# Modulation vectors by row sums on VectorE, state space weights on VectorE alone, and table loads counted as waits, in a two-layer diffusion backbone

## The chip, the cores and the metric

The kernel runs on one core of one Trainium2 chip. The metric is the device time of one execution in microseconds; the kernel before is shown with the median of three runs. A core has TensorE (matmuls, into PSUM), VectorE, ScalarE, GpSimd, and SyncE, which here issues every DMA. In the profile they are called PE (PEld is its loading of weights), DVE, ACT, POOL and SP.

## The reference

Two layers work on 384 tokens of 1024 features: 128 context tokens and 256 latent tokens. Each token set has a conditioning vector of its own, and each layer computes nine modulation vectors of 1024 from it, a shift, a scale and a gate for each of three sublayers:

```python
sc = jax.nn.silu(cond)
mod = sc @ w_ada[l] + b_ada[l]                    # 1024 -> 9 x 1024
sh1, sc1, g1, sh2, sc2, g2, sh3, sc3, g3 = split(mod, 9)
h = rmsnorm(x, norm_w[l, 0]) * (1 + sc1) + sh1
x = x + 0.5 * g1 * swiglu_a(h)                    # 1024 -> 2816 -> 1024
h = rmsnorm(x, norm_w[l, 1]) * (1 + sc2) + sh2
x = x + g2 * (concat(gla(h), delta_rule(h), s5(h)) @ w_out[l])
h = rmsnorm(x, norm_w[l, 2]) * (1 + sc3) + sh3
x = x + 0.5 * g3 * swiglu_b(h)
```

The third mixer (S5) is a diagonal state space in complex numbers. Its discretized weights (powers of the decay times b and c) depend on parameters alone, so they can be made before the mixer runs. All is in float32.

## The kernel before

**Tiling.** Activations lie transposed: a tile is 128 features by 384 tokens. Each 128x128 piece of a weight is multiplied in three passes: activations and weights are each split into a high and a low half that together have the accuracy of float32 (`mm3`: high x high, high x low, low x high). Each weight tile of 128x1024 thus needs ScalarE, which casts `raw` to its high half `wh`, and VectorE, which subtracts to get the low half `wl`. There are three `raw`, two `wh` and two `wl` tiles. TensorE needs about four microseconds for one tile.

**Stages.** The program runs FFN (0,0), mixer 0, FFN (0,2), FFN (1,0), mixer 1, FFN (1,2); the first number is the layer, the second the sublayer. An FFN has 22 products of gate and up (16 matmul triples each), each followed by SiLU, a product, and a split into `ph` and `pl`, and then 8 down projections of 22 triples. A norm stands between stages.

**Modulation.** The vectors are numbered by block (0 to 8 in each layer). The first two are made at the start on TensorE. The table `ADA` says for every stage which vectors it makes on the side (`now`) and which late (`late`). A side vector goes through `ada_side`: 8 loads of 128x1024 of `w_ada` (rows are inputs), and for each of the two conditionings an accumulation on VectorE, `asum <- araw * sT + asum`; the first of the eight is a scaled copy on ScalarE. What is left is a sum over partitions, which `ada_sum` does on TensorE with 8 matmuls against a one-hot constant; `ada_end` then copies on ScalarE, transposes twice on TensorE and adds the bias on VectorE. A late vector is multiplied whole on TensorE with 32 small matmuls, held back until the stage's last product, so that they fill TensorE while the norm runs. Eleven vectors are made on the side and five late; two of the late ones, (0,8) and (1,8), belong to the mixers.

**State space weights.** In the FFN ahead of each mixer, `s5_prep` makes powers and `s5_weights` makes, in four quarters, products of 128x512 and writes them to DRAM. `s5_weights` uses `self.vp`, an engine handle for which the planner may choose VectorE or GpSimd at each instruction.

**Order.** Every operation is recorded with the engines that it may run on, a planned cost and what it depends on; the planner `Plan` sets the order of each engine's queue with clocks of its own. It takes the operation that can start first (`when`), and among those that can start within 100 ns of it on the same engine the one of highest priority. Modulation's side work has the lowest priority (`side=-1`), the weight stream a high one (20). A function of another table set on ScalarE adds 1300 to the planned cost `c`, not to the planned start. `pace` and `calm` hold back the loads of side vectors by the FFN's progress and by the planned load of the DMA queue. Engines carry out their queues in order, so an instruction that waits holds back all behind it.

**Tiles.** `place` gives out the tiles of side work: six `araw` and three `asum` of 128x1024. The two running sums of a side vector are held `asum` tiles; the state space weights take theirs from `asum` as well.

## Time and profile before

| | |
|---|---|
| median of 3 runs | 1878.63 us (1873.07 to 1885.66) |
| profiled execution | 1874.38 us, its span from first to last instruction 1872.6 us |
| TensorE | busy 1794.6 us, granted clock 0.988 on average |
| VectorE, ScalarE, GpSimd | busy 1257.7, 791.4 and 294.3 us |
| chain that ended last | TensorE 72%, VectorE 16%, ScalarE 4%, DMA 4%, issue 3%, GpSimd 1% |

The chain that ended last is followed back from the end: at each step to what released the instruction, or to the one before it on its engine. 72% of it is TensorE, so TensorE sets the pace; where VectorE stands in it, TensorE waited for VectorE. A matmul's length is modelled, so that a busy TensorE can still have small gaps; the distance of equal instructions in the timeline tells more. All recorded operations have line 552, that of the planner's call, so groups are told apart by tile names: `wl<-raw,wh` is the low half of a weight, `s<-s,ps` and `pl<-s,ph` belong to a product of gate and up, `asum<-araw,sT,asum` is modulation's accumulation, `s5T` belongs to the state space weights.

### The profile page before, as it was taken

The page shows a single profiled execution, that of the slowest core. Times are in us where ns is not written, and L with a number is a line of the kernel's source. Part 1 is how long each engine was busy: PE and PEld are TensorE (multiplying, and loading weights), DVE is VectorE, ACT ScalarE, POOL GpSimd, SP SyncE. Part 2 cuts the span into 40 slices and gives each one's busy share as a digit, 9 for nine tenths or more (in the row PEclk, how much of TensorE's full clock was granted, in tenths as well). Part 3 has the DMA queues.
Part 4 walks back from the last instruction along what each step waited for, and adds up shares of the span by engine and source line. Part 5 has one row for each costly group of instructions (what it writes and reads, how often), then busy time and mean ns, then how long its engine had stood idle before and what let it go on. Part 6 is the DMA issues. An engine that isn't in the chain of part 4 may idle for free.

```text
span 1872.6 us, 33567 instructions
## 1 busy us (share of the span) xinstructions
PE 1794.6 (96%) x13626; PEld 1639.7 (88%) x13626; DVE 1257.7 (67%) x2061; ACT 791.4 (42%) x1357; POOL 294.3 (16%) x350
## 2 busy tenths in 40 slices
PE   8999999998999999999999999999999999999998
PEld 6988899887786779999988999997877768999997
DVE  4898885577895767666559777645989667444333
ACT  4533332465434553333254433335564355333332
POOL 1133240125110010000013125102342001000000
PEclk9999999999999999999999999999999999999999
DMA  9766677343110435556635565663421104333443
GB/s 285 264 211 205 221 237 240 116 146 110 49 35 24 158 113 181 194 167 192 226 124 175 188 207 190 199 218 131 134 87 49 35 23 170 124 124 125 129 124 96
DMA packets 111835, 282.05 MB, mean 151 GB/s; under 512 B 22656, under 2 KB 41408, under 8 KB 111680
## 3 DMA queue, kind: packets, MB, share of 16 engines
q1 hardware_dynamic: 111680, 279.90, 46.1%
q8 instruction: 107, 1.75, 0.4%
q14 instruction: 48, 0.39, 0.1%
HBM read 266.37 MB, written 13.48 MB: 149 GB/s over the span
## 4 chain that ended last, share of the span: by engine, by line
PE 72%; DVE 16%; ACT 4%; DMA 4%; issue 3%; POOL 1%; SPq 0%; DVEq 0%; POOLq 0%; ACTq 0%
PE ps L552 72%; DVE wl L552 4%; DVE asum L552 3%; DVE mM L552 2%; DVE s L552 2%; DMA araw<-in_wada 2%; DVE mZ L552 1%; ACT s L552 1%; DVE Ga L552 1%; ACT wh L552 1%; ACT h L552 1%; DMA wd<-asum 1%; DVE Gb L552 1%; DMA kd<-sC 0%; ACT mZ L552 0%
## 5 line engine op out<-in xcount | busy, mean ns | idle before, releaser
L552 ACT CAST wh<-raw 128x1024 fp32r<-128x1024 f32 (+1 forms) x332 | 341.7, 1030 | 701.6 <-PE ps L552 546.6
L552 PE MATMUL ps<-h,wl 128*128 128x384 f32 x1792 | 611.4, 341 | 15.0 <-DVE wl L552 14.5
L552 PE MATMUL ps<-h,wh 128*128 128x384 f32 x1792 | 612.8, 342 | 11.4 <-ACT h L552 9.9
L552 PE MATMUL ps<-l,wh 128*128 128x384 f32 x1792 | 610.9, 341 | 4.9 <-DVE l L552 3.9
L552 DVE TENSOR_TENSOR wl<-raw,wh 128x1024 fp32r<-128x1024 f32 (+1 forms) x332 | 414.0, 1247 | 264.2 <-ACT wh L552 263.8
L552 PEld LDWEIGHTS ps<-h,wl 128*128 128x128 f32 x1792 | 340.5, 190 | 25.3 <-DVE wl L552 21.7
L552 PEld LDWEIGHTS ps<-h,wh 128*128 128x128 f32 x1792 | 340.6, 190 | 23.2 <-ACT h L552 14.2
L552 PEld LDWEIGHTS ps<-l,wh 128*128 128x128 f32 x1792 | 340.4, 190 | 13.1 <-DVE l L552 9.3
L552 DVE SCALAR_TENSOR_TENSOR asum<-araw,sT,asum 128x1024 f32<-128x1024 f32 x154 | 204.8, 1344 | 57.4 <-DMA araw<-in_wada 56.7
L552 PE MATMUL ps<-ph,wl 128*128 128x384 f32 x704 | 237.6, 337 | 1.9 <-DVE wl L552 1.8
L552 PE MATMUL ps<-ph,wh 128*128 128x384 f32 x704 | 237.8, 338 | 0.0
L552 PE MATMUL ps<-pl,wh 128*128 128x384 f32 x704 | 237.4, 337 | 0.0
L552 PEld LDWEIGHTS ps<-ph,wl 128*128 128x128 f32 x704 | 132.2, 188 | 3.7 <-DVE wl L552 2.8
L552 PEld LDWEIGHTS ps<-ph,wh 128*128 128x128 f32 x704 | 132.2, 188 | 0.9 <-issue 0.6
L552 PEld LDWEIGHTS ps<-pl,wh 128*128 128x128 f32 x704 | 132.2, 188 | 0.4 <-issue 0.4
L552 POOL TENSOR_TENSOR s<-x,s 128x384 f32<-128x384 f32 x24 | 25.1, 1054 | 566.1 <-ACT s L552 520.2
L552 DVE TENSOR_TENSOR s<-s,ps 128x384 f32<-128x384 f32 x88 | 48.4, 551 | 79.4 <-PE ps L552 76.4
L552 PE MATMUL ps<-mZ,mM 64*64 64x128 f32 (+1 forms) x960 | 67.5, 267 | 6.9 <-DVE mM L552 4.0
L552 PEld LDWEIGHTS ps<-mZ,mM 64*64 64x64 f32 x960 | 53.2, 134 | 21.8 <-DVE mM L552 9.6
L552 ACT CAST ph<-s 128x384 fp32r<-128x384 f32 x88 | 44.6, 509 | 49.8 <-DVE s L552 49.6
L552 DVE SCALAR_TENSOR_TENSOR s<-s,p_small,s 128x392 f32<-128x392 f32 x96 | 61.9, 661 | 2.7 <-ACT s L552 1.8
L552 POOL TENSOR_TENSOR asum<-s5T,s5T 128x512 f32<-128x512 f32 x20 | 39.0, 1948 | 157.6 <-PE ps L552 99.0
(303 smaller groups left out, 2081.9 us busy)
## 6 DMA issues: line engine op xcount, KB each, us to landing
raw<-in_wgu SPq DMA_DIRECT2D x170, 512.0 KB, 3.9
araw<-in_wada SPq DMA_DIRECT2D x106, 512.0 KB, 4.9
raw<-in_wdn SPq DMA_DIRECT2D x64, 512.0 KB, 3.6
raw<-in_win SPq DMA_DIRECT2D x44, 512.0 KB, 3.5
raw<-in_wdn SPq DMA_DIRECT2D x32, 384.0 KB, 3.2
raw<-in_wout SPq DMA_DIRECT2D x16, 512.0 KB, 3.5
araw<-in_wada SPq DMA_DIRECT2D x22, 256.0 KB, 5.8
bd<-s SPq DMA_DIRECT2D x16, 256.0 KB, 4.1
```

Source lines behind the costliest of these rows:

```text
L552: getattr(self.eng[e], fn)(*a, **kw)
```

## The change

It has four parts.

1. A side vector is computed the other way round. The input holds `w_ada` once more, transposed (`wadaT`: 128 outputs by 1024 inputs in each block), and both conditioning vectors repeated over all partitions (`cR`). At the start of each stage two tiles take SiLU of `cR`. For each of 8 blocks and each conditioning, one VectorE instruction multiplies the block by that tile and writes the row's sum into a column of `adav` (`accum_out`). One addition of the bias ends the vector. The sum over partitions, the copy on ScalarE, the two transposes and the two additions are gone. The product itself isn't used; it goes to a tile `trash` or over the block.
2. The table `ADA` changes: (0,8) and (1,3) become side vectors of FFN (0,2), and (1,8) one of FFN (1,2). The mixers make none. Late are (0,5) and (1,5) alone. Fourteen vectors are made on the side.
3. `s5_weights` runs on VectorE alone, and its tiles come from the six `araw`, since the three `asum` are now held by `trash` and the two SiLU tiles.
4. In `when`, a change of table set adds its 1300 to the planned start, not to the cost.

```diff
@@ _pack
     o["wada"] = f(g["w_ada"])
+    o["wadaT"] = f(g["w_ada"].reshape(L, D, 9, KD, 128).transpose(0, 2, 3, 4, 1))
+    o["cR"] = f(np.broadcast_to(cc.T[None], (128, 2, D)))
@@ Plan.when
             if w[3] is not None and w[3] != self.table:
-                c += 1300.0
+                s += 1300.0
@@
 ADA = {(0, 0): ([(0, 2), (0, 3), (0, 4), (0, 6), (0, 7)], [(0, 5)]),
-       (0, 1): ([], [(0, 8)]),
-       (0, 2): ([(1, 0), (1, 1), (1, 2)], [(1, 3)]),
+       (0, 2): ([(0, 8), (1, 0), (1, 1), (1, 2), (1, 3)], []),
        (1, 0): ([(1, 4), (1, 6), (1, 7)], [(1, 5)]),
-       (1, 1): ([], [(1, 8)]),
-       (1, 2): ([], [])}
+       (1, 2): ([(1, 8)], [])}
@@ Kern.ada_side
-        acc = [raw(KD + s, True) for s in range(2)]
-        for k in range(KD):
+        v = self.t(pool, [128, KD, 2], "adav")
+        for d in range(KD):
             yield pace
             yield self.plan.calm()
             self.adan += 1
-            t = raw(k)
-            self.dma(out=t, in_=self.A["wada"][l, k * 128:(k + 1) * 128, b * 1024:b * 1024 + 1024])
+            t = self.place(pool, 0, False)
+            self.dma(out=t, in_=self.A["wadaT"][l, b, d])
             for s in range(2):
-                if k == 0:
-                    self.act(acc[s], t, AF.Copy, scale=self.sT[:, k, s:s + 1])
-                else:
-                    self.ve.scalar_tensor_tensor(acc[s], t, self.sT[:, k, s:s + 1], acc[s], ALU.mult, ALU.add)
-        self.plan.spawn(self.ada_sum(l, b, acc), 5)
+                self.ve.scalar_tensor_tensor(t if s else self.trash, t, 1.0, self.silu[s], ALU.mult, ALU.mult,
+                                             accum_out=v[:, d, s:s + 1])
+        self.ve.tensor_tensor(self.mod[l][:, 8 * b:8 * b + 8, :], v,
+                              bc(self.bada[:, l, 8 * b:8 * b + 8], 2, [128, KD, 2]), ALU.add)
+        self.do(lambda: self.done.add(("ada", l, b)))
         yield
-    def ada_sum(self, l, b, acc):
...
-            for g in range(4):
-                self.pe.matmul(pa[32 * g:32 * g + 32, :], self.cst("hot")[:, 31 - s:63 - s],
-                               acc[s][:, g * 256:g * 256 + 256], start=s == 0, stop=s == 1)
@@ Kern.adas
+        yield pace
+        places = [self.place(pool, KD, True) for _ in range(3)]
+        self.trash, self.silu = places[0], places[1:]
+        for s in range(2):
+            self.dma(out=self.silu[s], in_=self.A["cR"][:, s])
+            self.act(self.silu[s], self.silu[s], AF.Silu)
@@ Kern.ada_plan
-            self.adan < RANK["pace"] * (self.prog - RANK["lead"]) * len(now) * KD / FT)
+        n = max(len(now), 3) * KD / FT
+        self.plan.spawn(self.adas(now, pool, lambda: self.adan < RANK["pace"] * (self.prog - RANK["lead"]) * n),
+                        RANK["side"])
@@ Mixer.s5_prep
-        z, d = k.place(fp, KD, True), k.place(fp, KD, True)
+        z, d = k.place(fp, 0, True), k.place(fp, 0, True)
@@ Mixer.s5_weights (z twice)
-        k, g = self.k, self.vp
+        k, g = self.k, self.ve
-            z = k.place(fp, KD, True)
+            z = k.place(fp, 0, True)
@@ program
-                            k.ada_plan(l, 1, mp, mx)
```

The parts move instructions at three places. The first is VectorE in FFN (0,0), behind the 14th product of gate and up (`s<-s,ps`); `wl` is the low half of a weight, `asum_1541` and `asum_1542` are a side vector's two sums. Before:

```order
L552 SCALAR_TENSOR_TENSOR asum_1542<-araw_1707,sT_89,asum_1542 128x1024
L552 SCALAR_TENSOR_TENSOR asum_1541<-araw_1802,sT_89,asum_1541 128x1024
L552 TENSOR_TENSOR wl_1495<-raw_1493,wh_1494 128x1024
L552 SCALAR_TENSOR_TENSOR asum_1542<-araw_1802,sT_89,asum_1542 128x1024
L552 TENSOR_TENSOR s_296_1794<-s_296_1794,ps_1700 128x384
```

The same place in the change; `asum_697` and `asum_698` are the SiLU tiles, `asum_696` is `trash`:

```order
L554 SCALAR_TENSOR_TENSOR asum_696,adav_1092<-araw_1592,asum_697 128x1024
L554 SCALAR_TENSOR_TENSOR araw_1592,adav_1092<-araw_1592,asum_698 128x1024
L554 TENSOR_TENSOR wl_1471<-raw_1469,wh_1470 128x1024
L554 TENSOR_TENSOR s5T_290_1778<-s5PW_869,p_s5c_742 128x512
L554 TENSOR_TENSOR s5T_291_1779<-s5PW_869,p_s5c_742 128x512
L554 TENSOR_TENSOR mod_1_75<-adav_1092,bada_84 128x16
L554 TENSOR_TENSOR araw_1777<-s5T_290_1778,s5T_291_1779 128x512
L554 TENSOR_TENSOR s_280_1742<-s_280_1742,ps_1645 128x384
```

Two accumulations for each load stay, with other operands; the products of the state space weights that GpSimd had now stand in VectorE's queue between two low halves, and a vector ends there with one addition.

The second is ScalarE at the end of mixer 0. `sZ` is the sigmoid of the state space part, `oss` the logarithm and exponential of the delta rule's norm, and `mM` and `mZ` feed matmuls. Before:

```order
L552 COPY h_836_5764<-ps_6201 128x512
L552 ACT_TABLE_LOAD
L552 ACTIVATE sZ_6033<-ps_6032,p_small_739 128x384
L552 ACTIVATE mZ_6434,oss_921_6433<-h_836_5764,rq_4370 128x128 x3
L552 CAST Gb_6369<-mZ_6371 128x4x128
L552 ACTIVATE mZ_6434,oss_921_6433<-h_836_5764,rq_4370 128x128
L552 ACTIVATE mM_6205<-ps_6204,scQ_3575 128x128
L527 ACT_TABLE_LOAD
L552 ACTIVATE oss_921_6433<-oss_921_6433,eps_88 128x4
```

In the change:

```order
L554 ACTIVATE mZ_6336,oss_904_6335<-h_819_5728,rq_4284 128x128 x4
L554 ACTIVATE mZ_6311<-ps_6310,kdS_3500 128x128
L554 ACTIVATE oss_904_6335<-oss_904_6335,eps_88 128x4
L554 ACTIVATE oss_904_6335<-oss_904_6335 128x4
L554 ACTIVATE mZ_6311<-ps_6310,kdS_3500 128x128
L554 ACT_TABLE_LOAD
L554 ACTIVATE sZ_5930<-ps_5929,p_small_739 128x384
```

Before, a third load and the second sigmoid stand eight rows further on. In the change both logarithms come ahead of the first sigmoid, and the second sigmoid follows seven rows on with no load of its own.

The third is TensorE at the end of mixer 0, behind the last product with the output weights (`Gb`). The two rows with `ones` are the norm's sum over features; the rows with `sT` are the late vector (0,8). Before:

```order
L552 MATMUL ps_6809<-Gb_6369,wl_5948 128x384
L552 MATMUL ps_6892<-s5X_6578,sT_89 32x256 x4
L552 MATMUL ps_6892<-s5H_6595,sT_89 32x256
L552 MATMUL ps_6822<-s_950_6686,ones_79 128x384
L552 MATMUL ps_6892<-s5H_6595,sT_89 32x256 x3
L552 MATMUL ps_6892<-kt_6611,sT_89 32x256 x2
L552 MATMUL ps_6822<-s_973_6810,ones_79 128x384
L552 MATMUL ps_6892<-kt_6611,sT_89 32x256 x2
L552 MATMUL ps_6892<-vt_6648,sT_89 32x256 x4
L552 MATMUL ps_6892<-Ga_6682,sT_89 32x256 x16
L552 MATMUL ps_6989<-h_977_6825,wh_6021 128x384
```

In the change:

```order
L554 MATMUL ps_6720<-Gb_6243,wh_5823 128x384 x2
L554 MATMUL ps_6720<-Gb_6243,wl_5824 128x384
L554 MATMUL ps_6733<-s_928_6600,ones_79 128x384
L554 MATMUL ps_6733<-s_951_6721,ones_79 128x384
L554 MATMUL ps_6867<-h_955_6736,wh_5917 128x384
```

Nothing is left between the norm's two sums and the first product of the next FFN. The order before has 50 table loads in all, that of the change 38.

## Rows read from the trace of the kernel before

**Rows 1.** The page, part 1: span; busy time, share and instructions of each engine

```profile
span 1872.6 us, 33567 instructions
PE 1794.6 (96%) x13626; PEld 1639.7 (88%) x13626; DVE 1257.7 (67%) x2061; ACT 791.4 (42%) x1357; POOL 294.3 (16%) x350
```

**Rows 2.** Timeline of DVE in FFN (0,2): start us, length us, what, [idle before]

```profile
757.42 0.56 DVE L552 TENSOR_TENSOR s<-s,ps 128x384 f32<-128x384 f32 x1 [0.66 <-PE ps L552]
...
767.19 0.56 DVE L552 TENSOR_TENSOR s<-s,ps 128x384 f32<-128x384 f32 x1 [1.95 <-PE ps L552]
...
770.52 2.48 DVE L552 SCALAR_TENSOR_TENSOR asum<-araw,sT,asum 128x1024 f32<-128x1024 f32 x2 [0.81 <-DMA araw<-in_wada]
...
775.51 0.56 DVE L552 TENSOR_TENSOR s<-s,ps 128x384 f32<-128x384 f32 x1 [1.36 <-PE ps L552]
```

**Rows 3.** Stretches: us, busy PE, PEld, DVE, ACT, POOL (x), clock, DMA share, GB/s

```profile
67.68:242.27 174.59, 165.34 (x1002) 156.41 (x1000) 159.96 (x236) 67.33 (x92) 58.03 (x50) 0.99 0.66 217
242.27:343.20 100.93, 99.40 (x598) 95.31 (x598) 63.00 (x81) 32.58 (x41) 15.03 (x12) 1.00 0.69 222
973.50:1167.18 193.68, 187.79 (x1137) 180.98 (x1138) 153.28 (x250) 79.95 (x110) 58.50 (x53) 1.00 0.60 195
1167.18:1263.00 95.82, 95.82 (x573) 93.67 (x571) 52.87 (x67) 29.68 (x38) 8.78 (x5) 1.00 0.64 206
681.93:860.15 178.22, 178.08 (x1046) 176.00 (x1047) 111.83 (x124) 67.92 (x94) 0.00 (x0) 1.00 0.54 181
...
1595.22:1770.52 175.30, 175.16 (x1010) 174.89 (x1011) 73.03 (x88) 60.96 (x86) 0.00 (x0) 1.00 0.39 127
1770.52:1862.50 91.98, 91.98 (x530) 91.45 (x528) 35.62 (x47) 27.09 (x33) 0.00 (x0) 1.00 0.37 108
```

**Rows 4.** DVE's groups in 681.93:860.15 (FFN (0,2)): count, busy us, mean ns, idle before

```profile
L552 DVE TENSOR_TENSOR wl<-raw,wh 128x1024 fp32r<-128x1024 f32 x43 | 52.6, 1224 | 24.7 <-ACT wh L552 24.7
L552 DVE SCALAR_TENSOR_TENSOR asum<-araw,sT,asum 128x1024 f32<-128x1024 f32 x32 | 40.5, 1282 | 21.5 <-DMA araw<-in_wada 21.5
...
L552 DVE TENSOR_TENSOR pl<-s,ph 128x384 fp32r<-128x384 f32 x21 | 11.6, 552 | 0.0
```

**Rows 5.** Timeline of ACT near the end of mixer 0

```profile
606.19 0.19 ACT L552 ACTIVATION_READ_ACCUMULATOR mZ<-h,rq 128x1 f32 x1
```

**Rows 6.** The page, part 6: DMA issues, count, KB each, us to landing

```profile
raw<-in_wgu SPq DMA_DIRECT2D x170, 512.0 KB, 3.9
araw<-in_wada SPq DMA_DIRECT2D x106, 512.0 KB, 4.9
```

**Rows 7.** Timeline of DVE in FFN (0,0)

```profile
158.31 1.29 DVE L552 TENSOR_TENSOR s5T<-s5PZ,p_s5b 128x512 f32<-128x512 f32 x2
```

**Rows 8.** DVE's groups in 67.68:242.27 (FFN (0,0))

```profile
L552 DVE SCALAR_TENSOR_TENSOR asum<-araw,sT,asum 128x1024 f32<-128x1024 f32 x52 | 71.9, 1393 | 5.1 <-DMA araw<-in_wada 5.0
L552 DVE TENSOR_TENSOR wl<-raw,wh 128x1024 fp32r<-128x1024 f32 x36 | 48.9, 1360 | 0.8 <-ACT wh L552 0.8
L552 DVE TENSOR_TENSOR pl<-s,ph 128x384 fp32r<-128x384 f32 x18 | 13.5, 752 | 0.0
```

**Rows 9.** POOL's groups in the same stretch

```profile
L552 POOL TENSOR_TENSOR s5T<-s5PW,p_s5c 128x512 f32<-128x512 f32 x12 | 18.4, 1549 | 0.4
```

**Rows 10.** Timeline of PE behind the last product of mixer 0: the norm's sums

```profile
662.09 0.91 PE L552 MATMUL ps<-s,ones 128*128 128x384 f32 x2
...
663.91 0.91 PE L552 MATMUL ps<-s,ones 128*128 128x384 f32 x2
```

**Rows 11.** Stretches of 2 us behind mixer 0 and behind mixer 1

```profile
677.00:679.00 2.00, 1.92 (x12) 1.84 (x12) 1.90 (x6) 1.98 (x4) 0.00 (x0) 1.00 0.00 0
...
1588.00:1590.00 2.00, 2.00 (x8) 2.00 (x7) 1.86 (x7) 2.00 (x6) 0.00 (x0) 0.50 0.00 0
```

**Rows 12.** Timeline of ACT near the end of mixer 0

```profile
609.52 1.28 ACT L552 ACT_TABLE_LOAD   x1
```

**Rows 13.** One stretch of 4 us near the end of mixer 0

```profile
612.00:616.00 4.00, 3.07 (x29) 1.52 (x28) 2.32 (x7) 3.97 (x14) 0.00 (x0) 1.00 0.00 0
```

39 lines of the change are left out of this document (8 added, 31 removed).

## The prediction

> **What bounds the kernel now.** I read the page's busy shares first, then the busy times of each engine in stretches cut at layer boundaries, then the groups of instructions inside single stretches, and last the timeline at the places that the change touches. TensorE is busy for 96% of the span and VectorE for 67% [rows 1], but a busy matmul is a modelled length, so I measure TensorE by pitch instead. In a stretch with no modulation work, successive products of gate and up end 8.32 us apart, and where one side vector's sum comes between, 9.77 us apart: one sum costs TensorE 1.45 us [rows 2]. So FFN (1,2), which has no modulation, is the floor: 175.3 us from the first product to the 22nd, and 92.0 us for the down projection [rows 3]. Against it FFN (0,2) stands 2.9 us longer in gate and up, which is just its two sums. The two FFNs that also prepare the state space weights are far longer: FFN (1,0) takes 193.7 us, 18.4 over the floor, and FFN (0,0), counted from its fourth product on, takes 174.6 us for 18 products, where 18 x 8.32 = 149.8: 24.8 over [rows 3]. In its down projection it is 8.9 over and (1,0) 3.8. Together that is 56.0 us over the floor, of which eight sums are 11.6; the other 44 are small state space matmuls, which stay, and waits for weights. VectorE says why: it is busy 160.0 of 174.6 us in FFN (0,0) and 153.3 of 193.7 in FFN (1,0), and in the same stretches GpSimd is busy 58 us [rows 3].
>
> **Part 1, the row sums.** Eleven side vectors lose their sum on TensorE (8 matmuls against the one-hot constant, a copy on ScalarE, 2 transposes): 11 x 1.45 = **-15.9 us**. VectorE also loses the wait that stands before the two additions of each. In exchange VectorE gets 16 instructions of 128x1024 for each vector where it had 14, and three vectors more, so 224 for 154. One costs 1.28 us by its row where nothing disturbs it [rows 4], and 1.20 more when it follows another (two take 2.48 [rows 2]). No row shows the new form, which also writes a sum. Nothing lets it be cheaper than the old form, so the lower end of that extra price is 0; the nearest row is ScalarE's own reading of an accumulator, 0.19 us [rows 5], of which part lies under the instruction behind. I take 0.1 us and keep 0 to 0.19; far outside lies a second pass over the data, 1.28 us, which is a rival below.
>
> [...]
>
> The loads change shape too, from rows of a wide matrix to whole blocks. Today's take 4.9 us to land, the contiguous weight blocks 3.9 [rows 6]; I count nothing for it, since VectorE's waits for them are short where it is busy. Eight blocks more for the two conditioning vectors and eight SiLUs on ScalarE lie under FFNs where ScalarE is half idle: nothing; without that cover eight times about a microsecond.
>
> **Part 2, state space weights on VectorE alone.** In FFN (0,0) the order gives VectorE 30 instructions of 128x512 between the fourth and the 22nd product where it had 10, and 18 where it had 5 behind them; in FFN (1,0) 36 for 14 and 12 for 1. Two of them take 1.29 us [rows 7], so 0.6 each: 20 x 0.6 + some 2 us of small copies = 14 us in the first stretch. Against this stands what GpSimd costs VectorE today. In that stretch the accumulation takes 1393 ns, the low half of a weight 1360 and the low half of a product 752 [rows 8]; where GpSimd is idle they take 1282, 1224 and 552 [rows 4]. 52 x 0.111 + 36 x 0.136 + 18 x 0.200 = 14.3 us. The move pays for itself almost exactly, and GpSimd's own 1549 ns instructions [rows 9] leave the chain.
>
> So VectorE's work after: FFN (0,0), first stretch, 160.0 - 14.3 + 14 - 1.2 (51 accumulations for 52) + 51 x 0.1 = **163.6 us** in 174.6; its down projection 63.0 + 13 x 1.2 + 13 x 0.6 + 2.9, less 3 of disturbance, = 86 in 100.9; FFN (1,0) 153.3 - 14.4 (the same 0.25 us for each of GpSimd's 58.5) + 6 x 1.2 + 22 x 0.6 + 1 + 3.8 = 164 in 193.7; FFN (0,2), which takes five vectors in place of three, 111.8 + 30 x 1.2 + 6.2 = 154 in 178.2. Nowhere does VectorE's work exceed today's wall time, but in FFN (0,0) it exceeds the 149.8 of the big products, so waits for weights remain there. I put the sum's 1.45 us as won everywhere, 2 us more in FFN (0,0), and give back 2 us in FFN (0,2), 1 in (1,0), and 0.5 in (1,2), whose single vector is 16 instructions in a VectorE that is 58% idle: **+1.5 us**.
>
> **Part 3, vectors moved out of the mixers and the FFN ends.** The 32 matmuls that filled TensorE behind the last product of both mixers and of FFN (0,2) are gone. They sat between the two matmuls of the norm, whose second began 1.8 us after the first [rows 10]; without them it can begin about 1 us sooner. On the other side they kept TensorE active. [...] I expect 0.50 in all three places and take **0 us**, between -3 (three times the earlier norm) and +6 (three times some 2 us at half clock).
>
> **Part 4, table loads count as waits.** The order falls from 50 loads to 38, five fewer in each mixer and two in FFN (1,0). Each is 1.28 us by its row [rows 12]. Most lie where ScalarE has room. At the end of each mixer it has none (3.97 of 4 us busy [rows 13]) and TensorE waits for it; there three loads become one. 2 mixers x 2 x 1.28 = **-5.1 us**; 0 if the planner's other order puts a later chain in their place, -10 if more of the ten reach the path.
>
> **Sum.** -15.9 + 1.5 + 0 - 5.1 = -19.5 us. Against the profiled execution's 1874.4 us that is 1855; that execution lies 4.3 us under the median of the runs, against which it would be 1859. I name 1857.
>
> **Rivals.** *VectorE takes it back* (same). If the accumulator costs the full 0.19 us and VectorE's 14.6 idle microseconds in FFN (0,0) stay as they are (they are waits at the head of its queue: loads, TensorE, GpSimd), its first stretch needs 168 + 14.6 = 183 us, 8 more than today; FFN (1,0) and (0,2) some 3 each. -15.9 - 5.1 + 14 gives about 1870. For it speaks that everything behind a waiting accumulation, the low weight halves above all, waits too and TensorE has only two of those ahead; against it that GpSimd's share of those waits goes. *VectorE's waits vanish* (faster, beyond the forecast): FFN (0,0) falls to its 163.6 us and (1,0) by 6 more: about 1842. *VectorE stands for its loads* (slower): in FFN (0,2) it waits 21.5 us for 16 loads today [rows 4], 1.3 each. If that stays, 31 loads there cost 42 us on top of its 154: 196, 18 over today's stretch; and 25 loads in FFN (0,0) cost 33 on top of 163.6: 197, 22 over. With FFN (1,0) and the mixers as forecast that gives about 1905. It decides from (175 - 154)/31 = 0.7 us a load in the one and (174.6 - 163.6)/25 = 0.4 in the other. Against it: where VectorE is busy, in FFN (0,0), 26 loads cost it only 5.1 us [rows 8], 0.2 each, so these waits are what idle time looks like. *The row sum runs at half rate* (slower): 1.28 us more for each; FFN (0,0)'s two stretches grow by about 49 and 19 us, (1,0)'s by 15, (0,2)'s by 49: 2000. *The change doesn't do what it says*: only if a sum's 1.45 us were cover for something else; the pitch in FFN (0,2) excludes that.
>
> **How the numbers follow.** Forecast 0.47, waits vanish 0.10, VectorE takes it back 0.31, stands for its loads 0.07, half rate 0.05. One per cent is 19 us, about what a measurement of this kernel can tell from no change, and the forecast lies right at that edge: it and the waits-vanish case split as 0.42 faster and 0.15 same; the take-back case is same but for 0.03 slower and 0.03 faster. Faster 0.45, same 0.40, slower 0.15. The forecast's own range, with the bounds of parts 2 to 4, is 1843 to 1868; the range that holds 8 in 10 reaches into the cases on both sides, 1834 to 1886.
>
> **What would show it.** No one-hot matmuls; FFN (0,2)'s pitch at 8.32 all through, else it stands for its loads; the row sum at 1.28 to 1.47 us; the low half of a product back at 552 ns in FFN (0,0), whose first stretch should last 165 to 173 us; VectorE at 95% or more there; 38 table loads, and the end of each mixer 2 to 3 us shorter; clock 0.50 behind both mixers. A row sum above 1.6 us, or a first stretch above 180 us, makes the forecast wrong.

## The result and the profile after

The changed kernel takes 1828.92 us (median of 4 runs, 1825.01 to 1834.65) where the kernel before, run beside it, takes 1876.88 (1873.07 to 1885.66): a ratio of 0.974 with a 95% interval of 0.970 to 0.979, or 48 us less. The forecast was 20 us less. The direction is right, the size is missed by more than double, and the time lies 14 us under the low end of the forecast's own range (1843) and 5 under that of the wider one (1834). Measured a second time, beside other runs, the same kernel came out at 1836.87 us and a ratio of 0.977 (0.973 to 0.980).

The profiled execution of the changed kernel took 1827.39 us. Its page, part 1 (compare [rows 1]; line 554 is now the planner's call):

```profile
span 1825.6 us, 32957 instructions
PE 1761.9 (97%) x13230; PEld 1624.1 (89%) x13230; DVE 1330.2 (73%) x2432; ACT 761.0 (42%) x1317; POOL 165.4 (9%) x259
```

VectorE has 72 us more to do and GpSimd 129 less. The stretches that answer to [rows 3], with the same columns: FFN (0,0) from its fourth product to its 22nd, its down projection, FFN (1,0), and FFN (0,2).

```profile
67.45:226.31 158.86, 156.10 (x924) 152.44 (x923) 155.01 (x313) 59.04 (x81) 10.55 (x14) 1.00 0.70 236
226.31:322.24 95.93, 95.43 (x581) 93.54 (x580) 81.50 (x138) 30.27 (x38) 0.00 (x0) 1.00 0.73 246
938.11:1123.50 185.39, 183.20 (x1095) 178.88 (x1096) 158.84 (x318) 71.26 (x101) 7.95 (x14) 1.00 0.62 211
651.58:827.68 176.10, 175.63 (x1010) 174.99 (x1011) 142.07 (x214) 64.18 (x87) 0.00 (x0) 1.00 0.65 224
```

In the first of them VectorE is busy for 98% of the time and TensorE too, and GpSimd's 58 us are down to 11. The table gives every stage of both profiled executions, measured in VectorE's timeline from `s<-s,ps` rows and from the last residual (`x<-ps,ghalf,x`) of an FFN to the first product of the next; so a down projection ends half a microsecond earlier here than in [rows 3].

| stage, us | before | changed | difference |
|---|---|---|---|
| FFN (0,0), 4th to 22nd product | 174.6 | 158.9 | -15.7 |
| its down projection | 100.4 | 95.9 | -4.5 |
| mixer 0 with both norms | 339.3 | 329.3 | -9.9 |
| FFN (0,2), products and down | 271.1 | 267.2 | -3.9 |
| FFN (1,0), products and down | 289.1 | 279.1 | -10.0 |
| mixer 1 with both norms | 332.7 | 331.3 | -1.4 |
| start, norm behind (0,2), FFN (1,2) | 354.9 | 353.3 | -1.6 |

A second profile of the changed kernel (at the end of the experiments) repeats FFN (0,0) and (1,0), but has FFN (0,2) at 270.9 us and the mixers at 332.8 and 334.3; so the 3.9 us of FFN (0,2) and much of the mixers' difference are not shown by these two columns alone.

VectorE's groups in FFN (0,0)'s first stretch (compare [rows 8]): line, engine, operation, tiles and shapes, count, busy us, mean ns, idle time before them.

```profile
L554 DVE TENSOR_TENSOR wl<-raw,wh 128x1024 fp32r<-128x1024 f32 x36 | 43.9, 1219 | 0.1
L554 DVE SCALAR_TENSOR_TENSOR asum<-araw,asum 128x1024 f32<-128x1024 f32 x26 | 31.7, 1218 | 1.1 <-DMA araw<-in_wadaT 1.1
...
L554 DVE TENSOR_TENSOR pl<-s,ph 128x384 fp32r<-128x384 f32 x18 | 9.9, 552 | 0.0
...
L554 DVE DVE_READ_ACCUMULATOR asum<-araw,asum 128x1 f32 x26 | 2.1, 82 | 0.0
```

The disturbance by GpSimd is gone (1219 for 1360 ns, 552 for 752). The row sum takes 1218 ns, less than the old accumulation's undisturbed 1282 [rows 4], and its reading of the accumulator is a row of its own. In the timeline:

```profile
99.75 1.22 DVE L554 SCALAR_TENSOR_TENSOR asum<-araw,asum 128x1024 f32<-128x1024 f32 x1
100.89 0.08 DVE L554 DVE_READ_ACCUMULATOR asum<-araw,asum 128x1 f32 x1
100.89 1.22 DVE L554 TENSOR_TENSOR wl<-raw,wh 128x1024 fp32r<-128x1024 f32 x1
```

The next instruction starts 1.14 us behind the row sum, at the same time as the reading: the accumulator costs nothing that the timeline shows, since a plain low half of a weight is followed 1.14 us behind it too (from 105.51 to 106.65). The transposed blocks land no faster than the old rows did (5.0 us for 4.9 [rows 6]), and in FFN (0,2) the waits for 31 of them are as long as for 16 before (22.2 us, [rows 4] has 21.5):

```profile
araw<-in_wadaT SPq DMA_DIRECT2D x112, 512.0 KB, 5.0
...
L554 DVE SCALAR_TENSOR_TENSOR asum<-araw,asum 128x1024 f32<-128x1024 f32 x31 | 37.9, 1223 | 22.3 <-DMA araw<-in_wadaT 22.2
```

### The profile page after: what moved, and what is told of

The parts are those of the page before. It is cut to its first block, busy times and chain, and to the rows that moved or that the text cites. A ratio compares the mean times of both kernels' runs of the same rounds, so it can differ in the third digit from the quotient of the medians.

```text
span 1825.6 us, 32957 instructions
## 1 busy us (share of the span) xinstructions
PE 1761.9 (97%) x13230; PEld 1624.1 (89%) x13230; DVE 1330.2 (73%) x2432; ACT 761.0 (42%) x1317; POOL 165.4 (9%) x259
## 4 chain that ended last, share of the span: by engine, by line
PE 75%; DVE 15%; ACT 3%; issue 3%; DMA 2%; SPq 1%; POOL 1%; DVEq 0%; POOLq 0%; ACTq 0%
PE ps L554 75%; DVE wl L554 4%; DVE s L554 2%; DVE araw L554 1%; DVE mM L554 1%; DVE asum L554 1%; ACT s L554 1%; DMA araw<-in_wadaT 1%; DVE mZ L554 1%; DMA araw<-in_wada 1%; SPq L554 1%; DVE s5T L554 1%; DVE h L554 1%; ACT wh L554 1%; DVE Ga L554 1%
## 5 line engine op out<-in xcount | busy, mean ns | idle before, releaser
L554 DVE TENSOR_TENSOR wl<-raw,wh 128x1024 fp32r<-128x1024 f32 (+1 forms) x332 | 404.7, 1220 | 210.6 <-ACT wh L554 209.8
L554 DVE SCALAR_TENSOR_TENSOR asum<-araw,asum 128x1024 f32<-128x1024 f32 x112 | 136.8, 1221 | 49.1 <-DMA araw<-in_wadaT 48.8
L554 DVE SCALAR_TENSOR_TENSOR araw<-araw,asum 128x1024 f32<-128x1024 f32 x112 | 136.7, 1220 | 1.2
L554 POOL TENSOR_TENSOR s<-x,s 128x384 f32<-128x384 f32 x24 | 24.8, 1040 | 887.4 <-ACT s L554 842.0
L554 PE MATMUL ps<-mZ,mM 64*64 64x128 f32 (+1 forms) x960 | 71.8, 268 | 1.1 <-DVE mM L554 0.9
```

The source lines that it names most:

```text
L554: getattr(self.eng[e], fn)(*a, **kw)
```

## The experiments

Each kernel is compared with the kernel before, run beside it on the same chip; ratios have 95% intervals. "Stage" numbers are those of the table above, from each kernel's own profile.

### State space weights on VectorE: undone, and alone

```diff
 def s5_weights(self, fp):
-        k, g = self.k, self.ve
+        k, g = self.k, self.vp        # e3_s5_either, in the changed kernel
-        k, g = self.k, self.vp
+        k, g = self.k, self.ve        # e4_s5_only, in the kernel before
```

> The changed kernel with the state space weights on VectorE or GpSimd again, as the planner chooses (67 of their 96 large instructions go to GpSimd). Theory A: in FFN (0,0) VectorE sets the pace in the changed kernel (155.0 of 158.9 us busy), and what GpSimd takes from it, it gives back by disturbing it, so its first stretch stays within 4 us and the kernel within 5: 1829 to 1834 us. Theory C: the prediction missed because GpSimd's part in the waits was far larger than the disturbance that it counted; then FFN (0,0) and (1,0) go back by 6 and 5 us: 1840 us or more.

Measured: 1863.49 us, ratio 0.992 (0.989 to 0.995). FFN (0,0)'s first stretch goes from 158.9 back to 177.4 us, FFN (1,0)'s from 185.4 to 199.6: theory C, by about three times its sizes.

> The kernel before with the state space weights on VectorE alone (96 large instructions there for 30). Theory A: on VectorE as it was (160.0 of 174.6 us busy in FFN (0,0)) the move pays for itself: FFN (0,0)'s first stretch stays within 4 us of 174.6, the low half of a product falls back from 752 to 552 ns, the kernel stays at 1872 to 1880 us. Theory C (GpSimd's waits were the larger part of the gain): 1866 us or less, with 6 us or more gone in FFN (0,0) and some 5 in FFN (1,0).

Measured: 1861.19 us, ratio 0.990 (0.987 to 0.994). Theory A falls twice, and with it the prediction's step. One line is worth 18 us in the kernel before, and 29 to 34 in the changed one (0.992 against 0.977 and 0.974). The two stretches of the kernel with the one line alone, FFN (0,0) and FFN (1,0):

```profile
69.58:235.16 165.58, 162.88 (x1006) 155.27 (x1005) 159.98 (x270) 67.36 (x92) 10.57 (x14) 1.00 0.70 230
...
963.06:1152.52 189.46, 186.74 (x1133) 179.91 (x1134) 153.12 (x279) 79.04 (x110) 7.44 (x14) 1.00 0.60 200
```

VectorE's busy time is 159.98 us, before it was 159.96 [rows 3]: the sum of work came out as the prediction had it, disturbance against moved instructions, to a fiftieth of a microsecond (so near a match is chance). Yet the stretch is 9.0 us shorter. Most of what went is waiting: TensorE was idle for 9.3 us and is for 2.7, VectorE for 14.6 and is for 5.6. The other 2.5 us are TensorE's busy time, at a granted clock of 0.99 before and 1.00 here. The waits of that stretch (who waited for whom: us, times, longest), first of the kernel before, then of the one with the line alone:

```profile
PEld ps L552 <- DVE wl L552: 9.8, 9, 2.2
PE ps L552 <- DVE wl L552: 6.7, 5, 1.9
...
DVE mod L552 <- PE ps L552: 4.1, 2, 2.7
...
DVE s5T L552 <- POOL asum L552: 2.1, 2, 1.2
```

```profile
PEld ps L552 <- DVE wl L552: 3.6, 7, 1.0
...
PE ps L552 <- DVE wl L552: 1.4, 3, 0.7
```

So 2.1 us of VectorE's idle time before were waits for GpSimd's own results; they left with the move, as the 4.1 us of waits for TensorE did. Where the waits lay is seen when the stretch of the kernel before is cut at its 18 products, of which these are seven (columns as in [rows 3]):

```profile
105.28:117.27 11.99, 10.87 (x73) 9.55 (x72) 11.85 (x33) 4.71 (x7) 0.00 (x0) 1.00 0.65 225
...
126.72:134.88 8.16, 6.15 (x31) 5.81 (x31) 8.16 (x8) 2.90 (x4) 4.36 (x3) 0.91 0.44 144
...
164.24:174.76 10.52, 9.49 (x55) 9.17 (x54) 9.65 (x11) 3.03 (x5) 6.59 (x3) 1.00 0.53 182
174.76:185.66 10.90, 9.40 (x55) 9.09 (x54) 9.78 (x9) 3.01 (x4) 5.17 (x6) 1.00 0.52 163
...
194.97:204.27 9.30, 8.93 (x61) 7.51 (x60) 6.35 (x12) 4.54 (x7) 3.37 (x3) 1.00 0.52 173
204.27:214.37 10.10, 10.10 (x62) 9.77 (x61) 6.79 (x10) 3.72 (x5) 2.14 (x2) 1.00 0.92 294
...
232.63:242.27 9.64, 9.30 (x56) 8.98 (x54) 9.64 (x11) 3.75 (x6) 7.78 (x3) 1.00 0.65 202
```

From 164.24 and from 174.76 on GpSimd is busy for 6.6 and 5.2 us, VectorE is behind, and TensorE stands idle for 1.0 and 1.5 us. From 194.97 and from 204.27 on VectorE is idle for 3.0 and 3.3 us, with nothing to make good. From 126.72 on TensorE is idle for 2.0 us and its granted clock is 0.91; with the one line alone it is 1.00 in all 18 products. Not every product fits: from 105.28 on TensorE is idle for 1.1 us without GpSimd, and from 232.63 on for 0.3 us with GpSimd busy for 7.8. That GpSimd's work beside VectorE makes the stage longer is what the runs show. That its disturbance comes in bursts, paid back over the stretch in busy time but not in time, is the reading that fits most of these rows; no run isolates it.

With the row sums it is worse. In the run with the line undone (e3_s5_either), the same two stretches and VectorE's groups of the first:

```profile
67.94:245.30 177.36, 163.73 (x953) 157.35 (x952) 175.20 (x305) 59.97 (x83) 62.05 (x48) 0.98 0.69 222
...
963.74:1163.35 199.61, 188.19 (x1095) 181.19 (x1095) 162.01 (x284) 71.41 (x101) 75.19 (x63) 0.98 0.59 195
```

```profile
L554 DVE TENSOR_TENSOR wl<-raw,wh 128x1024 fp32r<-128x1024 f32 x36 | 49.2, 1366 | 0.0
L554 DVE SCALAR_TENSOR_TENSOR araw<-araw,asum 128x1024 f32<-128x1024 f32 x31 | 43.7, 1411 | 0.2
```

A row sum takes 1411 ns, and VectorE is busy for 175.2 of 177.4 us. The planner put 62 row sums into this stretch, 11 more than in the changed kernel, so the fair measure is the whole FFN (0,0), both stretches: 274.7 us here, 254.8 in the changed kernel and 275.0 before. All that TensorE saved is lost again.

### Work on GpSimd that is not on the path

```diff
 def ada_side(self, l, b, pool, pace):
                 self.ve.scalar_tensor_tensor(t if s else self.trash, t, 1.0, self.silu[s], ...
                                              accum_out=v[:, d, s:s + 1])
+                for _ in range(2):
+                    self.po.tensor_tensor(self.gd, self.silu[0][:, 0:192],
+                                          v[:, d, s:s + 1].to_broadcast([128, 192]), ALU.mult)
```

> The changed kernel with two GpSimd products of 128x192 behind each row sum, for which nothing waits: about 1 us of GpSimd for each, some 50 to 60 in FFN (0,0)'s first stretch (58 before). Theory D, disturbance: each us of GpSimd costs VectorE 0.25 to 0.4 us (14.3 us for 58 before, some 20 for 62 with the state space weights on either engine), and where VectorE is busy 155.0 of 158.9 us all of it is paid: FFN (0,0) 172 to 180, FFN (1,0) 187 to 192, FFN (0,2), where VectorE has 34 us to spare, 176 to 179: 1845 to 1858 us. Theory W: what GpSimd cost was that VectorE and TensorE waited for its slow instructions; work for which nobody waits then costs 0 to 4 us: 1829 to 1833.

Measured: 1888.72 us, ratio 1.004 (1.001 to 1.006), no faster than the kernel before: theory D, and beyond its range. One product took 1.1 us of GpSimd, so that there was twice as much of it as planned. FFN (0,0)'s first stretch and FFN (0,2):

```profile
68.79:244.58 175.79, 165.73 (x955) 157.54 (x955) 171.93 (x303) 60.11 (x83) 106.39 (x104) 0.98 0.64 210
...
687.58:875.68 188.10, 179.59 (x1015) 175.60 (x1016) 165.25 (x212) 65.18 (x87) 145.56 (x122) 1.00 0.62 210
```

The first is 16.9 us longer than in the changed kernel, and the down projection behind it another 11.0. The second is 12.0 us longer though VectorE is idle for 23 us of it: GpSimd's 146 us cost VectorE 23.2 us (165.3 less 142.1), 0.16 for each, and half of that reached the path. VectorE waited 1.8 and 3.5 us for GpSimd itself in the two (the next vector's `adav` waits for it), which leaves disturbance for the rest. How it comes about, in VectorE's timeline of FFN (0,2), while GpSimd runs without a pause:

```profile
752.58 1.51 DVE L554 TENSOR_TENSOR wl<-raw,wh 128x1024 fp32r<-128x1024 f32 x1
754.02 0.54 DVE L554 TENSOR_TENSOR s<-s,ps 128x384 f32<-128x384 f32 x1
754.48 1.21 DVE L554 SCALAR_TENSOR_TENSOR araw<-araw,asum 128x1024 f32<-128x1024 f32 x1
...
755.62 0.85 DVE L554 TENSOR_TENSOR pl<-s,ph 128x384 fp32r<-128x384 f32 x1
756.40 1.53 DVE L554 SCALAR_TENSOR_TENSOR asum<-araw,asum 128x1024 f32<-128x1024 f32 x1
```

```profile
748.70 15.46 POOL L554 TENSOR_TENSOR gd<-asum,adav 128x192 f32<-128x192 f32 x12 [1.35 <-DVE asum L554]
```

Most instructions that meet GpSimd are 0.30 us longer whatever their length (1.51 for 1.22, 0.85 for 0.55), and some get through unharmed (1.21 from 754.48 on). (With GpSimd's products of 128x512 in FFN (0,0) of the kernel before, a single `wl` took up to 2.08 us.) `s<-s,ps`, which reads PSUM, is not longer (0.54, 0.55 in the changed kernel). What makes the delay the rows don't show; it is not a wait for the whole of the other's instruction, since a GpSimd product takes 1.29 us there (15.46 us for 12) and the delay is 0.30.

### The row sum's price

```diff
                                              accum_out=v[:, d, s:s + 1])
+                self.ve.tensor_copy(self.trash[:, 0:128], self.silu[0][:, 0:128])
```

> The changed kernel with a copy of 128x128 on VectorE behind each of the 224 row sums, some 0.15 us each: the row sum at the price that the prediction gave it (1.30 us for 1.14). If VectorE sets the pace in FFN (0,0), its first stretch takes the whole of 51 x 0.15 = 7.6 us (158.9 to 166.5), the down projection 0 to 2; FFN (1,0), where VectorE is busy 158.8 of 185.4 us, 1 to 2 of its 5.7; FFN (0,2) and (1,2) nothing: 1836 to 1841 us. If TensorE is the bound in FFN (0,0) (busy 156.1 of 158.9): 0 to 2 us there, 1829 to 1832.

Measured: 1839.45 us, ratio 0.976 (0.972 to 0.981), within the interval of the changed kernel. The median alone would fit the first expectation; the stages don't. FFN (0,0)'s two stretches, and the copies of the first:

```profile
68.22:227.47 159.25, 156.71 (x946) 153.34 (x945) 155.77 (x345) 59.62 (x83) 8.91 (x14) 1.00 0.70 232
227.47:324.08 96.61, 95.17 (x563) 93.37 (x561) 95.32 (x187) 30.83 (x37) 0.00 (x0) 1.00 0.67 214
```

```profile
L554 DVE COPY asum<-asum 128x128 f32<-128x128 f32 x44 | 9.8, 222 | 0.1
```

79 copies cost FFN (0,0) 1.1 us in all. The planner, which gives side work the lowest priority, left 45 row sums in the first stretch where it had 51, and put the others into the down projection, where VectorE had 14 us to spare. So the size of the row sum's price, which the prediction got wrong, moves nothing here. "VectorE is 98% busy" did not mean that it set the pace.

### The row sums: undone, and alone

```diff
 def s5_weights(self, fp):             # e5_rows_undone, in the kernel before
-        k, g = self.k, self.vp
+        k, g = self.k, self.ve
 def when(...):
-                c += 1300.0
+                s += 1300.0
```

> The kernel before with the state space weights on VectorE alone and the table rule of the change; modulation as before (sums on TensorE, late vectors in the mixers). Against the changed kernel this undoes the row sums and the moved vectors alone. If the parts add up, FFN (0,0)'s first stretch is that of the state space part alone, 165.6 us, FFN (1,0) 189.5, the mixers those of the table rule alone, 332.8 and 331.8: 1852 to 1855 us, so that the row sums are worth some 24 us when GpSimd is out of the way, where they were worth 9 with it (1872.5 less 1863.5). If the row sums are worth only those 9: 1838 us.

Measured: 1855.68 us, ratio 0.986 (0.981 to 0.991). The parts without the row sums add up as expected in the FFNs, (0,0) 164.5 us and (1,0) 190.3, and in mixer 1, 331.4; mixer 0 took 338.3 us where 332.8 was expected. From this kernel to the changed one the three FFNs with modulation and the norm between them lose 5.7 + 1.5 + 2.1 + 1.8 + 0.3 + 4.9 + 1.6 = 17.9 us (products and down projections in turn), against the second profile of the changed kernel 14.1: the 15.9 us of TensorE's eleven sums lie between the two.

The opposite kernel, e9_rows_alone, is the changed one with `self.vp` in `s5_weights` and `c += 1300.0` in `when`.

> The changed kernel with both other parts undone: the state space weights on VectorE or GpSimd, the table rule as before; only the row sums and the moved vectors are left. Theory E: the row sums need both other parts. Without the one, GpSimd's disturbance keeps VectorE full (FFN (0,0) 177 us, (1,0) 199, as in the run with only that undone); without the other, the mixers without late vectors run at a lower granted clock (0.95) and take 343 to 346 us each. TensorE's sums still go (-3 in (0,2), -6 at the small places). Sum against before: +3, +6, +4 and +13, -9: some 1885 to 1895 us against 1879, slower or the same. Theory F: the row sums stand by themselves for the 15.9 us of TensorE that the prediction gave them: 1860 to 1866 us.

Measured: 1890.66 us, ratio 1.006 (1.003 to 1.009). Theory E, within its range: the part that the change is named for makes the kernel 0.6% slower when it is made alone. FFN (0,0) and FFN (1,0):

```profile
67.53:251.11 183.58, 168.43 (x972) 160.99 (x970) 178.21 (x311) 60.06 (x83) 73.01 (x53) 0.97 0.66 217
...
978.76:1176.18 197.42, 187.79 (x1095) 181.88 (x1095) 162.79 (x285) 73.89 (x103) 73.26 (x63) 0.98 0.59 197
```

They are 9 and 4 us longer than before, with VectorE full in the first and GpSimd busy for 73 us in each; the mixers take 342.2 and 337.2 us, 3 and 5 more than before. FFN (0,0) lost more and the mixers less than theory E had, so the sum is in part luck. The twelve executions had mean granted clocks of 0.961 to 0.979, the kernel before beside it 0.978 to 0.991. At 0.977 and 0.979 this kernel took 1879.54 and 1880.65 us, at 0.978 the kernel before 1888.30 and 1891.14: the loss comes with a lower clock. In the profile the clock is 0.97 in FFN (0,0), where TensorE is idle for 15 us, and 0.95 and 0.96 in the mixers; what lowers it there isn't shown.

### The table rule: alone, and undone

```diff
 def when(...):
             if w[3] is not None and w[3] != self.table:
-                c += 1300.0
+                s += 1300.0          # e1_table_only, in the kernel before
-                s += 1300.0
+                c += 1300.0          # e2_table_undone, in the changed kernel
```

> The kernel before with one line changed: the planner adds a table load's 1300 ns to the start, not to the cost (50 table loads become 38). The changed kernel's two mixers, from the last residual of one FFN to the first product of the next, are 9.9 and 1.4 us shorter; cut at the first output product of the mixer, mixer 0 gained 6.9 us ahead of it and 3.0 behind, mixer 1 lost 3.5 ahead and gained 4.9 behind. Theory A: the rule acts only ahead of the cut (net -3.4), and what was won behind it (-7.9) comes from the missing late vectors: here 1873 us, mixers 332 and 336, each end behind the cut still 60 us. Theory B, the rule brings all of the mixers' 11 us: 1866 us, ends of 56 to 57 us. By the prediction's own term: -5.1, 1872 us.

Measured: 1872.53 us, ratio 0.995 (0.993 to 0.998): 8.8 us, between the prediction's 5.1 and its bound of 10. The mixers take 332.8 and 331.8 us, 6.5 and 0.9 less; the norms behind them stay as they were (21.7 and 20.5 us from the mixer's last residual, before 20.5 and 21.3), and in the changed kernel they are hardly shorter (20.7 and 19.4). The time is theory A's, but mixer 1 is as short as theory B has it, and the second profile of the changed kernel has mixers of 332.8 and 334.3; so the two theories can't be told apart.

> The changed kernel with the table rule as before (50 table loads). Theory A (rule worth 3.4 us, ahead of the cut alone): 1832 us, ends behind the cut still 56 to 57 us. Theory B (rule worth 11 us): 1840 us, ends of 60 us. By the prediction: +5.1, 1834 us. If the rule only reshuffles each mixer's order, mixer 0 may lose and mixer 1 gain, and the total stays within 4 us of 1829.

Measured: 1852.91 us, ratio 0.986 (0.982 to 0.990): no theory had it. The mixers in this run's profile take 343.4 and 345.5 us, 14 more each than in the changed kernel:

```profile
324.00:667.35 343.35, 318.30 (x3226) 261.04 (x3224) 251.85 (x487) 173.47 (x368) 73.03 (x109) 0.95 0.23 75
1238.05:1583.56 345.51, 321.35 (x3226) 263.42 (x3224) 251.74 (x488) 173.59 (x368) 72.97 (x109) 0.94 0.23 74
```

ScalarE's five table loads more, 1.28 us each, explain 6.4 us in each at most; what is new is a mean granted clock of 0.95 and 0.94 where the mixers of the kernel before have 0.97 and 0.98. The profiled execution, 1862.30 us at a mean clock of 0.973, is one of this run's longer ones. At 0.983 this kernel took 1848.77 us and the changed kernel 1834.65, 14 us apart as a whole, where the two mixers of the profiled execution are 28 us longer; so a part of these is the clock of that execution.

### Late vectors

```diff
 ADA = {(0, 0): ...                    # e6_late_back, in the changed kernel
-       (0, 2): ([(0, 8), (1, 0), (1, 1), (1, 2), (1, 3)], []),
+       (0, 1): ([], [(0, 8)]),
+       (0, 2): ([(1, 0), (1, 1), (1, 2)], [(1, 3)]),
        (1, 0): ([(1, 4), (1, 6), (1, 7)], [(1, 5)]),
-       (1, 2): ([(1, 8)], [])}
+       (1, 1): ([], [(1, 8)]),
+       (1, 2): ([], [])}
```

> The changed kernel with the old table of vectors: (0,8), (1,3) and (1,8) are late vectors on TensorE again, in the mixers' and FFN (0,2)'s ends; the eleven side vectors keep the new row sums. The norm behind each of the three places (last residual to first product) took 20.5, 21.3 and 20.5 us before and 20.7, 19.4 and 19.3 in the changed kernel. If the late vectors are all there is to part 3: 1.2 us more at each, less 2 us in FFN (0,2) and 0.3 in (1,2): 1829 to 1832 us. If they also cover table loads and keep the clock up inside the mixers (where undoing the table rule cost 14 us each without them, but only 6.5 and 0.9 with them): the mixers come out at 326 to 328 us and the kernel at 1822 to 1826.

Measured: 1835.74 us, ratio 0.975 (0.970 to 0.979), above both expectations but no difference from the changed kernel (0.974 and 0.977), as the prediction's 0 for part 3 said; the mixers are 333.0 and 334.5 us, so that no cover was lost with the late vectors. To see whether it is lost under the old table rule, both were undone together (this table, and `c += 1300.0`):

> The changed kernel with the old table of vectors (late vectors on TensorE in the mixers and in FFN (0,2)'s end) and the old table rule. Undoing the table rule alone made the mixers 14 us longer each (343.4 and 345.5 us, granted clock 0.95 and 0.94), putting the late vectors back alone 3 us (333.0 and 334.5, 0.98). Theory G: the old rule's order is slow only where the late vectors are missing; with both back the mixers are those of the kernel before, 339 and 333 us at 0.97 and 0.98: 1842 to 1846 us. Theory H: the old rule's order in the mixers is slow by itself beside the new parts, late vectors or not: 343 to 346 us each, 1852 us or more.

Measured: 1860.35 us, ratio 0.988 (0.985 to 0.992), mixers of 346.7 and 348.2 us: theory H. What takes so long there is seen in stretches of 2 us, the first of this kernel's mixer 1, the second of the kernel before at the like place of its mixer 0, behind the last large matmuls of the same chain:

```profile
1465.45:1467.45 2.00, 2.00 (x13) 1.30 (x13) 0.00 (x0) 0.81 (x2) 0.00 (x0) 0.50 0.00 0
```

```profile
570.67:572.67 2.00, 2.00 (x18) 1.31 (x19) 0.00 (x0) 0.46 (x2) 0.00 (x0) 1.00 0.28 115
```

TensorE works nearly alone there, at a granted clock of 0.50 in the one and of 1.00 in the other. It goes on for some 20 us (from 1463.45 on six such stretches in a row at 0.50, then 10 us at 0.62 on average), and costs some 10, as an estimate from the distance of equal matmuls in the kernel before: 0.32 us at a granted clock of 0.50, 0.17 at 1.00, in TensorE's timeline behind mixer 1:

```profile
1588.61 0.52 PE L552 MATMUL ps<-h,wl 128*128 128x384 f32 x1
1588.93 0.52 PE L552 MATMUL ps<-h,wh 128*128 128x384 f32 x1
1589.25 0.52 PE L552 MATMUL ps<-l,wh 128*128 128x384 f32 x1
...
1591.23 0.34 PE L552 MATMUL ps<-h,wl 128*128 128x384 f32 x1
1591.41 0.33 PE L552 MATMUL ps<-h,wh 128*128 128x384 f32 x1
1591.58 0.33 PE L552 MATMUL ps<-l,wh 128*128 128x384 f32 x1
```

In the 8 us ahead of the two stretches TensorE was busy for 1.8 to 2.0 of every 2 us in the one and 1.7 to 2.0 in the other. Why the clock was granted there in the one and not in the other, the rows don't show.

### How far one profile can be trusted

> The changed kernel once more, without an edit. It shows how far one profile's stages can be trusted: if the mixers (329.3 and 331.3 us in the first profile) come out within 1 us again, the differences of 3 to 4 us between the other runs' mixers are their edits'; if they come out at 332 to 338 us, these are the granted clock's. The FFNs' stretches should repeat within 1 us, the median within 1829 +- 4 us.

Measured: 1836.87 us, ratio 0.977 (0.973 to 0.980), a median 8 us above the first, outside what was expected. FFN (0,0) and (1,0) repeat to half a microsecond. FFN (0,2) takes 178.6 us for 176.1, and the mixers 332.8 and 334.3 for 329.3 and 331.3:

```profile
68.92:227.31 158.39, 156.09 (x921) 151.90 (x920) 154.99 (x311) 59.02 (x81) 10.57 (x14) 1.00 0.71 237
...
323.25:656.01 332.76, 313.69 (x3226) 257.73 (x3224) 249.15 (x489) 168.79 (x363) 68.01 (x108) 0.97 0.24 77
```

So a difference of 3 us in one mixer says nothing (with e5_rows_undone's mixer 0, not of 5 either), FFN (0,2) can be read to some 3 us, and FFN (0,0) and (1,0), which carry the argument, to the microsecond.

The clock goes with the time within each kernel: the kernel before, run beside the first four experiments, took 1872.79 us at a mean granted clock of 0.990 and 1892.42 at 0.976, e13_late_and_table 1846.70 at 0.986 and 1863.26 at 0.974. That is some 14 us for each hundredth, in kernels whose instructions are the same from one execution to the next.

### Tries for a faster version

All four start from the changed kernel. The first paces side vectors at 0.75 of the FFN's progress; the second also moves the last 14 GpSimd instructions of `s5_prep` to VectorE (one of them is shown); the third besides moves (1,4) into FFN (0,2) and makes (1,5) a side vector. The fourth has the second's move alone.

```diff
-RANK = dict(... pace=0.85, ...)
+RANK = dict(... pace=0.75, ...)
 def s5_prep(self, fp):
-            self.po.tensor_tensor(tt[0][:, q], B[:, q], bc(cf[:, 0], 2, sh), ALU.mult)
+            V.tensor_tensor(tt[0][:, q], B[:, q], bc(cf[:, 0], 2, sh), ALU.mult)
...
-       (0, 2): ([(0, 8), (1, 0), (1, 1), (1, 2), (1, 3)], []),
-       (1, 0): ([(1, 4), (1, 6), (1, 7)], [(1, 5)]),
+       (0, 2): ([(0, 8), (1, 0), (1, 1), (1, 2), (1, 3), (1, 4)], []),
+       (1, 0): ([(1, 5), (1, 6), (1, 7)], []),
```

> A try for a faster version: the changed kernel with side vectors paced at 0.75 of the FFN's progress in place of 0.85. The copies of the dose run showed that VectorE takes 18 us more in FFN (0,0) without time, most of it in the down projection. With fewer row sums in the first stretch of FFN (0,0) and (1,0) VectorE has room there: 2 to 4 us less in the first, 2 in the second, nothing lost elsewhere: 1823 to 1827 us. If what is left there over the floor is the small state space matmuls on TensorE (156.1 of 158.9 us busy): 1829.

> The same, with the last 14 GpSimd instructions of the state space preparation (10.6 us in FFN (0,0), 8.0 in FFN (1,0)) on VectorE as well. By the disturbance they cost VectorE some 3 us each time, by their place in the chain more: TensorE was idle for 1.9 us in each of the two products at which they stand. Expected: 1 to 3 us less in each of the two FFNs than the run before: 1818 to 1826 us. If only the sum of work counts: no difference.

> The same again, with vector (1,4) made in FFN (0,2), where VectorE has 34 us to spare, and (1,5) made on the side of FFN (1,0) in place of late on TensorE. The norm behind FFN (1,0) loses its 32 small matmuls, as three others did in the change (1.2 us each); FFN (0,2) has 16 row sums more, 18 us. Expected: 1 us less behind FFN (1,0), 0 to 2 more in FFN (0,2): within 2 us of the run before. If the fill kept the granted clock up at the start of mixer 1: 2 us more.

> A try for a faster version: the changed kernel at its own pace (0.85) with the last 14 GpSimd instructions of the state space preparation on VectorE. With the pace at 0.75 they brought some 2 us in each of FFN (0,0) and (1,0), and the slower pace cost 4 to 6 us in FFN (0,2). Expected: 1824 to 1829 us; if the two don't add up, 1829.

Measured: 1842.53, 1830.66, 1829.81 and 1830.82 us, ratios 0.979 (0.976 to 0.983), 0.974 (0.970 to 0.977), 0.973 (0.969 to 0.977) and 0.974 (0.971 to 0.976). None is shown to be faster than the changed kernel, and the first, second and fourth missed what was expected. The slower pace gained nothing in FFN (0,0) (160.7 us) and cost 4 to 6 us in FFN (0,2) (182.2 us; the changed kernel's two profiles have 178.6 and 176.1). The last one has the best FFN (0,0) of all, 155.7 us in its first stretch, 3.2 less than the changed kernel, but a mixer 1 of 338.1 at a granted clock of 0.94 in the same profile: its gain is smaller than what the clock gives and takes.

## Why the prediction was right or wrong

**The bound.** TensorE's pace with VectorE as the one it waits for: right in FFN (0,0) and (1,0). That waits made so much of the 44 us over the floor, and that they could go, was not seen: 24.8 us over in FFN (0,0)'s first stretch became 9.1 (158.9 less 18 x 8.32).

**Part 1, TensorE's sums.** Right: 15.9 us were forecast, 17.9 and 14.1 measured in the stages that have them (the changed kernel's two profiles against e5_rows_undone). They come only if GpSimd's disturbance is gone: with it, FFN (0,0) takes 274.7 us as a whole (e3_s5_either), as long as before.

**Part 1, the row sum's price.** Wrong in sign: instead of 0.1 us more, a row sum's successor starts 1.14 us behind it, 0.06 sooner than behind the old form, 1.20 [rows 2]. "Nothing lets it be cheaper than the old form" was the error; the old form has a scalar taken from a tile, the new one a constant, which may be the reason and was not tried. It made VectorE's forecast of 163.6 us in the first stretch 8.6 too high (155.0), and it cost no time: the dose run has that price and loses 1 us. A second pass over the data is not seen: the row sum takes 1218 to 1220 ns in FFN (0,0)'s first stretch, next to 1219 for a plain product of the size. So the half-rate rival is out.

**Part 2, the step that failed.** "The move pays for itself almost exactly" was worked out in VectorE's busy time and was right there, 159.98 against 159.96 us. It was then taken for the stage's time, with 2 us won and 3.5 given back. (The range's low end of 1843 leaves some 6 us for this part, since 1857 less 3 and 5 is 1849; the working doesn't say from what.) By e4_s5_only it wins 9.0 us in FFN (0,0)'s first stretch, 3.7 in its down projection and 3.6 in FFN (1,0), 16.3 in all, where the sum has a loss of 1.5. That difference of 18 us is the largest part of the miss, which is 28 us by the first measurement of the changed kernel and 22 by the second. What the step took for granted is that equal work means equal time. What it left out, as the rows read, is that disturbance comes in bursts, and that VectorE and TensorE, two weights apart, can't lend each other time: a burst stops TensorE, then VectorE stands waiting for TensorE (`mod<-ps` 4.1 us, none with the one line alone). VectorE's waits for GpSimd itself (2.1 us) went as well. The 14.6 idle microseconds of VectorE were looked at, in a rival that kept them as they were, though they were the sign of it. The give-backs in FFN (1,0) and (1,2) did not come either: (1,0) won 6.5 us from e5_rows_undone to the changed kernel, where three sums are 4.4, and (1,2)'s products take 175.0 us for 175.3. That in FFN (0,2) stays open: its 271.1 us became 267.2 in one profile and 270.9 in the other, where three sums are 4.4.

**Part 3.** Right: 0 us (e6_late_back). The granted clock behind the mixers was forecast at 0.50 in both places; it was 0.50 behind mixer 0 and 1.00 behind mixer 1, the other way round than before [rows 11]:

```profile
644.00:646.00 2.00, 2.00 (x8) 2.00 (x7) 1.95 (x6) 2.00 (x6) 0.00 (x0) 0.50 0.00 0
...
1545.00:1547.00 2.00, 2.00 (x14) 1.94 (x13) 0.70 (x2) 1.93 (x3) 0.00 (x0) 1.00 0.00 0
```

The 0.50 in all three places was the author's estimate; what sets the clock there no run shows. Nor does one show the 6 us at half clock that the range allowed for: the norms behind the three places take 20.7, 19.4 and 19.3 us in the changed kernel, 20.5, 21.3 and 20.5 before.

**Part 4.** Mis-sized, within its bound: -5.1 forecast, -8.8 alone, and -11.3 or -4.9 in the two profiles of the changed kernel and -2.3 in that of e5_rows_undone (both mixers together). Taken from the changed kernel it is worth some 20 us (0.986 for 0.974 or 0.977; 14 at a like mean clock), twice its bound of 10, and the old order's mixers then ran at a lower granted clock (0.95 and 0.94 in e2_table_undone). What sets that clock stays open: three kernels with row sums and the old rule have it (e2, e9, e13) and the two without row sums don't (before, e4), each in one profile, but with the new rule e14_prep_ve has 0.94 in mixer 1 and e8_gp_work 0.95 in mixer 0.

**The rivals.** "VectorE's waits vanish", with one chance in ten and 1842 us, was the right mechanism; with VectorE's true work of 155.0 for 163.6 us in FFN (0,0) and the mixers as measured it gives 1842 - 8.6 - 6.2 = 1827. So near is luck: the stretch took 158.9 us, not its work's 155.0, and the mixers' 6.2 us were not there in the second profile. "VectorE takes it back", with three in ten, is what happens without part 2 (e3, e9). "Stands for its loads" was wrong as argued against it: 31 loads cost what 16 did. "The change doesn't do what it says" did not come, since TensorE's sums were won; that the row sums alone lose (1890.66 us) has another reason than the cover that this rival named.

**The signs named.** Table loads (38), the low half of a product (552 ns) and VectorE at over 95% came true; the row sum lies under its 1.28 to 1.47 us, and the first stretch under its 165 to 173, both on the faster side. FFN (0,2)'s products are 176.1 / 21 = 8.39 us apart, 8.51 in the second profile, where 8.32 was forecast. The mixers' ends were not told apart from the rest of the mixers.

## What to carry to other kernels

What one engine's work does to another is not priced by adding the delays to the other's busy time: equal busy time was 9 us apart here. Where two engines depend on each other within a few instructions, a delay can, by the reading above, be paid at once and not be made good later, so look at the stage product by product, and treat idle time beside a full engine as something that can go. Parts of a change can need each other: the row sums, with the moved vectors, lose 10 us alone and win 18 to 23 beside the other two, so try a change's enabling part before judging the other. "98% busy" shows the bound only if the work in it can't move; low-priority work that a planner can put later isn't a bound.
